# Cached keys and values in another tile shape: 32 blocks by four tokens in place of 96 blocks by one, in a two-layer decoder step

## The chip, the cores and the metric

One Trainium2 chip, one core. The metric is the device time of one launch in microseconds (us), median over runs. A core has five engines with instruction queues of their own: TensorE (PE; PEld are its weight loads), VectorE (DVE), ScalarE (ACT), GpSimd (POOL) and SyncE (SP), which issues nearly all DMAs of this kernel.

## What is computed

One step of a two-layer decoder trunk for a prompt (256 tokens) and for samples (8 batches of 4 tokens), width 1024, all float32. The first layer mixes tokens with gated linear attention, the second with dilated attention: 16 heads of 64, three groups that look 128 steps back at dilations 1, 4 and 16, joined by their softmax denominators. The sample tokens attend to a cache of 2048 earlier keys and values per batch (8 MB of each per batch) and to their own four.

```python
DIL_WINDOWS, DIL_DILATIONS = (128, 512, 2048), (1, 4, 16)

def dilated_group_sample(q, k_ctx, v_ctx, dil, steps, wb):
    T = q.shape[1]
    idx = wb + np.arange(T)[:, None] - dil * np.arange(steps + 1)[None, :]
    kg = k_ctx[:, idx]
    vg = v_ctx[:, idx]
    s = jnp.einsum('bthe,btjhe->bhtj', q, kg) * DIL_SCALE
    p, lse = masked_softmax(s, jnp.asarray(idx >= 0)[None, None])
    return jnp.einsum('bhtj,btjhe->bthe', p, vg), lse.transpose(0, 2, 1)
```

With dilation 16, token t of the four needs the cache rows 16 j + t for the blocks j = 0 to 127. So of each block of 16 rows four are read, and each of the four matters to one token only. The last 32 blocks lie in the last 512 rows, which dilation 4 reads in full.

## The kernel before

The program is one long sequence of stages: adaLN products, feed-forward, linear attention, feed-forward, the shared keys and values, feed-forward, queries, dilated attention, output product, feed-forward. Each weight product is three TensorE products of high and low halves (L554 to L556); the halves come from ScalarE (L183) and VectorE (L187).

Weights and caches come through one `Stream`. `job_list` writes down every load of the program in order. A job is cut into pieces of at most 128 x 1024 floats, and `pump` issues a DMA from SyncE for the next piece as long as fewer than RAW_BUFS = 11 pieces are loaded or in flight past the last one released. A consumer calls `take`, reads, and `free` releases the slots, in order; that lets `pump` issue more. A slot is reused, so an issue waits for those that read its last contents.

The change is in `dilated`, in the part for the sample tokens, about 1123 to 1321 us of the profiled execution. It runs over 16 steps x (and five more for what lags): four passes of two batches each (`it`, called `pr` in the helpers; `bp` is the batch of the two), and in each pass four steps (g, tp). g = 1 is the last 512 rows of the cache as 128 blocks of four rows, g = 2 the first 1536 rows as 96 blocks of 16 (J2 = 96); tp is 0 or 1. Group 0's keys lie within those of g = 1. In every step, per batch:

- `cache_job` (L329 on) made the load: two tokens u (2 tp and 2 tp + 1) of every block, each a piece of its own with a block per partition. That is 128 partitions (512 KB) for g = 1 and 96 (384 KB) for g = 2, and rows of 4 KB in both.
- `keys` turned the raw tiles with TensorE transposes (L1393), 8 chunks of 128 columns for each token, four transposes into one PSUM bank, and evacuated each bank into `kt`, by turns on ScalarE (L1513) and VectorE (L1511). GpSimd appended the sample's own key as a last column (L1517).
- `key_scores` multiplied the queries (`qz`, four row groups of 32: head half by batch) with `kt` (matmuls of L1390 into bank `pb`); VectorE then added them up in `Sc` through `tmask`, which keeps for each query row its own token (L1550, L1552).
- After the four steps of a pass, `softmax` normalized `Sc` and spread group 1's weights by token into the tile `W` (tag W1, one buffer). `weights` turned `W` (four transposes), `Pn` (the sample's own) and the 96 columns of `Sc` for g = 2, and VectorE spread the latter by token with the constant `ptmask` (L1589), in a `scratch` tile (named xh or xl).
- `outputs`, five steps later than the keys, multiplied these weights with the value tiles (L1390, out pa, 512 columns, two instructions each), four row groups for each token; `om` and `selz` collect the result in `pd`.

Between the parts of a step, `pieces` puts in small parts of the prompt's attention (tiles `pe`, `pT`). All transposes and matmuls in here are pinned to the order in which they are written, so PE runs in program order. The loads of a step x are the keys of step x and the values of step x - 5.

Of the kernel before, what the change touches and what calls it, by code (L numbers as in the profile page):

```python
# [18 lines left out]
P = 128  # L19
# [33 lines left out]
def host_constants():  # L53
    c = {}
    c["ident"] = np.eye(P, dtype=np.float32)
    half = 32
    inv = (10000.0 ** (-np.arange(half) / half)).astype(np.float32)
    pos = np.concatenate([np.arange(NP), np.tile(PAST + np.arange(TS), NB)]).astype(np.float32)
    ang = (inv[:, None].astype(np.float32) * pos[None, :]).astype(np.float32)
    cos, sin = np.cos(ang).astype(np.float32), np.sin(ang).astype(np.float32)  # L60
    t = np.stack([np.concatenate([cos, cos]), np.concatenate([-sin, sin])])
    c["rope"] = np.ascontiguousarray(np.tile(t, (1, 2, 1)).transpose(1, 0, 2))
    c["ropeq"] = c["rope"] * np.float32(0.125)
    i = np.arange(P)
# [35 lines left out]
    c["ptmask"] = np.broadcast_to((np.arange(32)[None, :] % TS == np.arange(TS)[:, None]), (P, TS, 32)).astype(np.float32).copy()  # L100
# [14 lines left out]
class Stream:  # L115
# [22 lines left out]
    def load(self, v, j, k0, nk):  # L138
        if j["kind"] == "first":
            for m in range(2):  # L140
                self.nc.sync.dma_start(v[:, :, 256 * m:256 * m + 256], j["src"][:, k0:k0 + nk, m])
        else:
            self.nc.sync.dma_start(v, j["src"][:, k0:k0 + nk, :])

# [186 lines left out]
def cache_job(I, name, g, b, tp, key):  # L331
    c = I[name][b].rearrange("s h e -> s (h e)")
    if g == 1:
        v = c[1536:2048, :].rearrange("(j t) f -> j t f", t=4)
    else:

        v = c.rearrange("(j t) f -> j t f", t=16)[0:J2]
    return dict(kind="r", key=key, src=v[:, 2 * tp:2 * tp + 2, :], nk=2, nc=D, rows=v.shape[0])


def body(tc, I, O, C, dbg=None):
# [1020 lines left out]
    def dilated(KT, Vt, Vs, xh, xl):  # L1362
# [134 lines left out]

        def keys(pr, g, tp, bp):

            n = P if g == 1 else J2  # L1500
            ji, _, raw = S.take(("K", g, pr, tp, bp))
            kt = [sp.tile([P, 4, 2, n + 1], F32, name=nm("kt"), tag=q, bufs=SPLIT_BUFS) for q in ("hi", "lo")]
            for c2 in range(4):
                pt = bankA().rearrange("p (f u j) -> p f u j", f=2, u=2)[:, :, :, 0:n]
                for f in range(2):
                    c = 2 * c2 + f
                    for u in range(2):
                        transpose(pt[:, f, u, :], raw[u][:, P * c:P * c + P], ident[0:n, 0:n])
                dst = kt[c2 // 2][:, 2 * (c2 % 2):2 * (c2 % 2) + 2, :, 0:n]
                if c2 % 2:  # L1510
                    V.tensor_copy(dst, pt)  # L1511
                else:
                    A.activation(dst, pt, AF.Copy)  # L1513
            S.free(ji)
            n0 = NP + TS * (2 * pr + bp) + 2 * tp
            for q in range(2):
                G.tensor_copy(kt[q][:, :, :, n], KT[:, 4 * q:4 * q + 4, n0:n0 + 2])  # L1517
            return kt

        def key_scores(g, tp, kc, qz, Sc):  # L1520
            n = P + 1 if g == 1 else N2
            ps = bankB()
            quarters = [(hp, bp) for hp in range(2) for bp in range(2)]

            for c4 in range(4):
                for kind in range(3 if g == 1 else 1):
                    for hp, bp in quarters:
                        c, q = 4 * hp + c4, 32 * (2 * bp + hp)
                        k_ = kc[bp][hp][:, c4]
# [9 lines left out]
            if g == 1:  # L1539
# [5 lines left out]
            for u in range(2):  # L1545
                t = 2 * tp + u
                for o_, m, s_ in [(132, 129, 129 * u), (261 + N2, 32, 324 + 32 * u)] if g == 1 else [(261, N2, N2 * u)]:
                    src, dst = ps[:, s_:s_ + m], Sc[:, o_:o_ + m]
                    if t == 0:
                        V.tensor_scalar(out=dst, in0=src, scalar1=ld["tmask"][:, 0:1], scalar2=None, op0=ALU.mult)  # L1550
                    else:
                        V.scalar_tensor_tensor(out=dst, in0=src, scalar=ld["tmask"][:, t:t + 1], in1=dst, op0=ALU.mult,  # L1552
                                               op1=ALU.add)
# [23 lines left out]
        def weights(Sc, W):  # L1577
            p1 = bankA()
            for t in range(TS):
# [2 lines left out]
            A.activation(W1, p1.rearrange("p (t x) -> p t x", t=TS), AF.Copy)  # L1582
# [163 lines left out]
```

## Time and profile before

| | |
|---|---|
| median of 3 runs | 1606.9 us (1605.67 to 1610.69) |
| the profiled execution | 1601.49 us |
| its span, mean granted TensorE clock | 1599.7 us, 0.979 |
| instructions | 31842 |
| DMA over the whole span | 342.75 MB, mean 214 GB/s |
| cache loads | 64 of 512 KB and 64 of 384 KB |

The profile is of one execution. "Busy" is the time in which an engine had an instruction running; the chain of work that ended last is followed back from the last instruction, step by step, to what released each. An idle time belongs to the instruction that came after it, and names what ended it. In a row such as "L1393 PE MATMUL pa<-ident,raw 96*128 96x96 f32 x256" stand the line, engine, operation, output and inputs, partitions by columns of the weights, the shape of the moving tile, and the count; busy us and mean ns of one follow.

### The profile page before, as it was taken

How to read it: one execution, taken by the hardware profiler on the slowest of the kernel's cores; microseconds unless marked ns; L12 is line 12 of the kernel's file. 1: busy time of each engine (PE TensorE's matmuls, PEld its weight loads, DVE VectorE, ACT ScalarE, POOL GpSimd, SP SyncE). 2: the span in 40 equal slices, each digit the busy share in tenths (PEclk: the TensorE clock that was granted, in tenths of full speed). 3: DMA queues.
4: the chain of work that ended last, by engine and by line, in shares of the span. 5: the costliest groups of instructions: out<-in, count | busy, mean ns of one | idle time of the engine just before them, and what ended most of it. 6: DMA issues, size and time to landing. Idle time of an engine off the chain costs nothing.

```text
span 1599.7 us, 31842 instructions
## 1 busy us (share of the span) xinstructions
PE 1506.4 (94%) x12794; PEld 1343.4 (84%) x12794; DVE 914.4 (57%) x1902; ACT 723.6 (45%) x1173; POOL 217.0 (14%) x367
## 2 busy tenths in 40 slices
PE   6999999999889999998999999898998988999996
PEld 4999998798868999987999999797755637899995
DVE  3644446596785444467544454666665667745556
ACT  2444334745644443346444433477443344544432
POOL 0000030102321000303000004032521112200001
PEclk8999999999999999999999999998999999999998
DMA  9966775644856678755676676643799998555430
GB/s 303 323 222 227 246 249 159 225 154 154 297 168 227 221 226 282 245 177 185 230 250 211 211 261 203 191 130 111 230 288 304 297 292 284 169 173 162 153 98 30
DMA packets 238822, 342.75 MB, mean 214 GB/s; under 512 B 12744, under 2 KB 202386, under 8 KB 238675
## 3 DMA queue, kind: packets, MB, share of 16 engines
q1 hardware_dynamic: 236210, 333.41, 65.6%
q0 software_dynamic: 2048, 7.14, 1.2%
q8 instruction: 100, 1.64, 0.4%
q14 instruction: 48, 0.39, 0.1%
q10 hardware_dynamic: 416, 0.17, 0.0%
HBM read 332.42 MB, written 8.26 MB: 213 GB/s over the span
## 4 chain that ended last, share of the span: by engine, by line
PE 73%; DMA 10%; DVE 8%; ACT 5%; issue 2%; POOL 1%; SPq 0%; DVEq 0%; ACTq 0%; POOLq 0%
PE pa L554 20%; PE pa L555 20%; PE pa L556 20%; DMA raw<-in_cache_k_dram 6%; PE pd L471 4%; DMA raw<-in_cache_v_dram 2%; DVE lo L187 2%; PE pa L1393 2%; PE pb L1390 1%; ACT xm L792 1%; ACT xm L1303 1%; PE pa L1051 1%; DVE z L694 1%; ACT hi L183 1%; ACT xh L800 1%
## 5 line engine op out<-in xcount | busy, mean ns | idle before, releaser
L554 PE MATMUL pa<-xh,hi 128*128 128x288 f32 x1868 | 548.3, 301 | 17.2 <-ACT xh L800 9.9
L556 PE MATMUL pa<-xh,lo 128*128 128x288 f32 x1868 | 554.2, 298 | 4.6 <-DVE lo L187 4.5
L555 PE MATMUL pa<-xl,hi 128*128 128x288 f32 x1868 | 555.2, 298 | 0.6 <-DVE xl L1663 0.4
L187 DVE TENSOR_TENSOR lo<-raw,hi 128x1024 fp32r<-128x1024 f32 (+2 forms) x365 | 424.1, 1170 | 227.6 <-ACT hi L183 225.2
L183 ACT ACTIVATE hi<-raw 128x1024 fp32r<-128x1024 f32 x350 | 358.7, 1035 | 254.9 <-PE pa L555 237.1
L554 PEld LDWEIGHTS pa<-xh,hi 128*128 128x128 f32 x1868 | 349.5, 190 | 38.1 <-ACT xh L800 18.3
L556 PEld LDWEIGHTS pa<-xh,lo 128*128 128x128 f32 x1868 | 356.0, 191 | 7.6 <-DVE lo L187 6.2
L555 PEld LDWEIGHTS pa<-xl,hi 128*128 128x128 f32 x1868 | 356.2, 191 | 1.1 <-DVE xl L1663 0.7
L554 PE MATMUL pa<-hh,hi 128*128 128x288 f32 x704 | 209.8, 298 | 0.0
L556 PE MATMUL pa<-hh,lo 128*128 128x288 f32 x704 | 208.9, 297 | 0.0
L555 PE MATMUL pa<-hl,hi 128*128 128x288 f32 x704 | 208.3, 296 | 0.0
L888 DVE TENSOR_TENSOR sa<-pa,sa 128x288 f32<-128x288 f32 x88 | 39.6, 454 | 181.8 <-PE pa L556 177.3
L554 PEld LDWEIGHTS pa<-hh,hi 128*128 128x128 f32 x704 | 132.8, 189 | 4.7 <-issue 2.9
L556 PEld LDWEIGHTS pa<-hh,lo 128*128 128x128 f32 x704 | 132.6, 188 | 0.2
L555 PEld LDWEIGHTS pa<-hl,hi 128*128 128x128 f32 x704 | 132.6, 188 | 0.1
L889 ACT ACTIVATE hh<-sa 128x288 fp32r<-128x288 f32 x88 | 38.7, 445 | 136.6 <-DVE sa L888 133.7
L887 ACT ACTIVATE sa<-pa 128x288 f32<-128x288 f32 x88 | 34.9, 401 | 97.6 <-PE pa L556 97.6
L1393 PEld LDWEIGHTS pa<-ident,raw 128*128 128x128 f32 (+1 forms) x512 | 53.3, 146 | 26.3 <-issue 8.1
L471 PE MATMUL pd<-raw,cT 128*32 128x256 f32 x1008 | 73.9, 385 | 1.3 <-ACT adas L479 1.3
L1393 PE MATMUL pa<-ident,raw 128*128 128x128 f32 (+1 forms) x512 | 63.7, 274 | 9.4 <-DMA raw<-in_cache_k_dram 4.6
L616 POOL TENSOR_TENSOR z<-z,lnpiv 128x288 f32<-128x288 f32 x6 | 4.7, 806 | 484.4 <-ACT lnpiv L611 484.4
L1513 ACT ACTIVATE kt<-pa 128x512 f32<-128x512 f32 (+1 forms) x64 | 34.0, 541 | 69.1 <-PE pa L1393 61.5
(381 smaller groups left out, 1756.1 us busy)
## 6 DMA issues: line engine op xcount, KB each, us to landing
raw<-in_w_ffn_up_dram SPq DMA_DIRECT2D x172, 512.0 KB, 6.1
raw<-in_w_ada_dram SPq DMA_DIRECT2D x110, 512.0 KB, 5.7
raw<-in_w_ffn_down_dram SPq DMA_DIRECT2D x80, 512.0 KB, 4.9
raw<-in_cache_k_dram SPq DMA_DIRECT2D x32, 512.0 KB, 7.3
raw<-in_cache_v_dram SPq DMA_DIRECT2D x32, 512.0 KB, 10.6
raw<-in_w_in_a_dram SPq DMA_DIRECT2D x24, 512.0 KB, 4.8
raw<-in_w_q_b_dram SPq DMA_DIRECT2D x24, 512.0 KB, 3.7
raw<-in_cache_k_dram SPq DMA_DIRECT2D x32, 384.0 KB, 10.6
```

The costliest lines, as they stand in the source:

```text
L183: self.pin("act", self.nc.scalar.activation(hv, src, AF.Copy))
L187: self.pin("dve", self.nc.vector.tensor_tensor(out=lo[:, k, :], in0=src[:, k, :], in1=hv[:, k, :].bitcast(F32), op=ALU.subtract))
L471: x = T.matmul(ps[32 * q:32 * q + 32, :], lhsT=cT[:, k, :], rhs=raw[kk][:, 256 * q:256 * q + 256], start=(k == 0), stop=(k == DC - 1), til ...
L554: ins = [T.matmul(ps, lhsT=whi, rhs=xhi, start=first, stop=False), T.matmul(ps, lhsT=whi, rhs=xlo, start=False, stop=False), T.matmul(ps, ...
L555: T.matmul(ps, lhsT=whi, rhs=xlo, start=False, stop=False),
L556: T.matmul(ps, lhsT=wlo, rhs=xhi, start=False, stop=last)]
L694: pin("dve", V.tensor_tensor(out=z[:, c, :], in0=z[:, c, :], in1=self.rstd, op=ALU.mult))
L887: A.activation(sa, pa[:, 0:NT], AF.Silu)
L888: V.tensor_tensor(out=sa, in0=pu[:, 0:NT], in1=sa, op=ALU.mult)
L889: A.activation(hh[:, m, :], sa, AF.Copy)
L1393: pin("pe", T.transpose(*a))
L1513: A.activation(dst, pt, AF.Copy)
```

## The change

Group 2's loads take another shape. A tile now holds 32 blocks by their first four rows, so its 128 partitions are (block, token) pairs, 512 KB in runs of 16 KB. The 96 blocks of a batch make three tiles: step tp = 0 takes the first two, step tp = 1 the third. The bytes are the same; four pieces of 96 partitions become three of 128, for keys and for values, and 128 cache loads become 112.

In `keys` a bank then holds two chunks of two tiles (tp = 0) or four chunks of one (tp = 1), and the batch's own four keys are appended once, at tp = 1. In `key_scores` the columns of a step are 256 and 132 in place of 194 and 194; a column's token is its index modulo 4, so VectorE adds four strided parts of 64 or 33 columns per step, in place of two of 97. In `weights` VectorE first spreads the 96 columns of `Sc` by token with `tmask` into a new tile `w2` with tag W1, PE turns its three parts, and VectorE copies them to the `scratch` tile. `outputs` runs over three value tiles where it ran over four tokens. The constant `ptmask` and its load are gone. Group 1 is as before.

```diff
+        elif "tiles" in j:
+            self.nc.sync.dma_start(v[:, 0, :], j["tiles"][k0])
...
-        v = c.rearrange("(j t) f -> j t f", t=16)[0:J2]
-    return dict(kind="r", key=key, src=v[:, 2 * tp:2 * tp + 2, :], nk=2, nc=D, rows=v.shape[0])
+        return dict(kind="r", key=key, src=v[:, 2 * tp:2 * tp + 2, :], nk=2, nc=D)
+    v = c.rearrange("(j t) f -> j t f", t=16)
+    tiles = [v[32 * i:32 * i + 32, 0:TS, :] for i in ((0, 1) if tp == 0 else (2,))]
+    return dict(kind="r", key=key, tiles=tiles, nk=len(tiles), nc=D)
...
-            n = P if g == 1 else J2
-            kt = [sp.tile([P, 4, 2, n + 1], F32, name=nm("kt"), tag=q, bufs=SPLIT_BUFS) for q in ("hi", "lo")]
-            for c2 in range(4):
-                pt = bankA().rearrange("p (f u j) -> p f u j", f=2, u=2)[:, :, :, 0:n]
...
+            nu, n = len(raw), P + (0 if (g, tp) == (2, 0) else TS if g == 2 else 1)
+            kt = [sp.tile([P, 4, nu, n], F32, name=nm("kt"), tag=q, bufs=SPLIT_BUFS) for q in ("hi", "lo")]
+            nf = 4 // nu
+            for c2 in range(DC // nf):
+                pt = bankA().rearrange("p (f u j) -> p f u j", f=nf, u=nu)
...
+                parts = [(t, 261 + 64 * tp, ps[:, t:nc_:TS]) for t in range(TS)]
+            for t, o_, src in parts:
+                dst = Sc[:, o_:o_ + src.shape[1]]
...
-            transpose(pt[0:J2, P:2 * P], Sc[:, 261:261 + J2], ident)
-            W2 = scratch[1][0:J2, 1536:2048].rearrange("p (q t x) -> p q t x", q=4, t=TS)
-            V.tensor_tensor(out=W2, in0=bc(pt[0:J2, P:2 * P].rearrange("p (q x) -> p q x", q=4), 2, TS),
-                            in1=bc(ld["ptmask"][0:J2], 1, 4), op=ALU.mult)
+            w2 = tile("W1", [P, TS, P])[:, 0:3, :]
+            V.tensor_tensor(out=w2.rearrange("p i (j t) -> p (i j) t", t=TS), in0=bc(Sc[:, 261:261 + J2], 2, TS),
+                            in1=bc(ld["tmask"], 1, J2), op=ALU.mult)
+            for i in range(3):
+                transpose(pt[:, P * i + P:P * i + 2 * P], w2[:, i, :], ident)
+            W2 = scratch[1][:, 1536:1536 + 3 * P].rearrange("p (i x) -> p i x", i=3)
+            V.tensor_copy(W2, pt[:, P:4 * P].rearrange("p (i x) -> p i x", i=3))
...
-                    for u in range(2):
+                    for u in range(len(rr[0][2])):
...
-                            mm(po[32 * gr:32 * gr + 32, :], lhsT=W1[:, t, 32 * gr:32 * gr + 32] if g == 1 else W2[:, gr, t, :],
+                            mm(po[32 * gr:32 * gr + 32, :], lhsT=(W1 if g == 1 else W2)[:, t, 32 * gr:32 * gr + 32],
```

SyncE's queue in the second pass, where the keys of step (2, 1) and the values of step (2, 0) of the pass before are issued. The number in a name only tells the tiles apart. Before:

```order
L143 DMA raw_12963<-in_cache_v_dram 128x1024
L143 DMA raw_12965<-in_cache_k_dram 96x1024
L143 DMA raw_12967<-in_cache_k_dram 96x1024
L143 DMA raw_12969<-in_cache_k_dram 96x1024
L143 DMA raw_12997<-in_cache_k_dram 96x1024
L143 DMA raw_12999<-in_cache_v_dram 96x1024
L143 DMA raw_13114<-in_cache_v_dram 96x1024
L143 DMA raw_13116<-in_cache_v_dram 96x1024
L143 DMA raw_13128<-in_cache_v_dram 96x1024
L143 DMA raw_13130<-in_cache_k_dram 128x1024
```

The same place now:

```order
L144 DMA raw_12937<-in_cache_v_dram 128x1024
L142 DMA raw_12939<-in_cache_k_dram 128x1x1024
L142 DMA raw_12941<-in_cache_k_dram 128x1x1024
L142 DMA raw_12943<-in_cache_v_dram 128x1x1024
L142 DMA raw_12971<-in_cache_v_dram 128x1x1024
L142 DMA raw_12973<-in_cache_v_dram 128x1x1024
L142 DMA raw_13086<-in_cache_v_dram 128x1x1024
L144 DMA raw_13088<-in_cache_k_dram 128x1024
```

Four key tiles of 96 partitions became two of 128; of the values this step still takes four, and the step after takes two.

PE's queue at `weights`, with the semaphores that an instruction waits for. Before:

```order
L1393 MATMUL pa_13571<-ident,pe_13234 128x128 x2
L1393 MATMUL pa_13577<-ident,W_916_13337 128x128 [waits DVE_49]
L1393 MATMUL pa_13577<-ident,W_916_13337 128x128 x3
L1393 MATMUL pa_13583<-ident,Pn_12243 128x128 [waits Activation_49]
L1393 MATMUL pa_13583<-ident,Sc_12664 96x128
L1390 MATMUL pd_12242<-om_13427,c_selz_11195 32x256 x4
L1390 MATMUL pa_13593<-raw_13298,xh_12235 32x512 [waits DMAHW0_49,DVE_49,Activation_49]
```

Now, where `W_939` is the tile w2:

```order
L1396 MATMUL pa_13509<-ident,pe_13178 128x128 x2
L1396 MATMUL pa_13515<-ident,W_908_13283 128x128 [waits DVE_49]
L1396 MATMUL pa_13515<-ident,W_908_13283 128x128 x3
L1396 MATMUL pa_13521<-ident,Pn_12241 128x128 [waits Activation_49]
L1396 MATMUL pa_13521<-ident,W_939_13525 128x128 [waits DVE_49,Activation_49]
L1396 MATMUL pa_13521<-ident,W_939_13525 128x128 x2
L1393 MATMUL pd_12240<-om_13365,c_selz_11193 32x256 x4
L1393 MATMUL pa_13535<-raw_13211,xh_12233 32x512 [waits DMAHW1_49]
```

The one transpose of `Sc`, without a wait, became three of w2, and the first of them waits for VectorE.

VectorE's queue at the same place. Before:

```order
L1511 COPY kt_13533<-pa_13541 128x4x128 [waits PE_49]
L1511 COPY kt_13534<-pa_13553 128x4x128 [waits PE_49]
L1589 TENSOR_TENSOR xl_12236<-pa_13583,c_ptmask_11191 96x512 [waits Activation_49]
L1511 COPY kt_13610<-pa_13618 128x4x96 [waits PE_49]
L1511 COPY kt_13611<-pa_13630 128x4x96 [waits PE_49]
```

Now:

```order
L1516 COPY kt_13471<-pa_13479 128x4x128 [waits PE_49]
L1516 COPY kt_13472<-pa_13491 128x4x128 [waits PE_49]
L1604 TENSOR_TENSOR W_939_13525<-Sc_12632,c_tmask_11187 128x384 [waits PE_49]
L1609 COPY xl_12234<-pa_13521 128x384 [waits PE_49,Activation_49]
L1516 COPY kt_13552<-pa_13560 128x512 [waits PE_49]
L1516 COPY kt_13553<-pa_13572 128x512 [waits PE_49]
```

One masked product of the turned weights became a product ahead of PE's transposes, which waits for PE, and a copy behind them; two kt copies stand ahead of it.

More of the change, by code (lines that the diff above doesn't have):

```diff
@@ L99, in host_constants @@
     c["rmask"] = np.repeat((i[:, None] // 64 == np.arange(2)[None, :]).astype(np.float32)[:, :, None], TS, axis=2)
-    c["ptmask"] = np.broadcast_to((np.arange(32)[None, :] % TS == np.arange(TS)[:, None]), (P, TS, 32)).astype(np.float32).copy()
     c["blkmask"] = ((i[:, None] % 32) // TS == np.arange(512)[None, :] // 64).astype(np.float32)
@@ L334, in cache_job @@
         v = c[1536:2048, :].rearrange("(j t) f -> j t f", t=4)
-    else:
-        v = c.rearrange("(j t) f -> j t f", t=16)[0:J2]
-    return dict(kind="r", key=key, src=v[:, 2 * tp:2 * tp + 2, :], nk=2, nc=D, rows=v.shape[0])
+        return dict(kind="r", key=key, src=v[:, 2 * tp:2 * tp + 2, :], nk=2, nc=D)
+    v = c.rearrange("(j t) f -> j t f", t=16)
+    tiles = [v[32 * i:32 * i + 32, 0:TS, :] for i in ((0, 1) if tp == 0 else (2,))]
+    return dict(kind="r", key=key, tiles=tiles, nk=len(tiles), nc=D)
 def body(tc, I, O, C, dbg=None):
@@ L1379, in dilated @@
         ld = {}
-        for n, sh in (("g0mask", [P, TS, 33]), ("tmask", [P, TS]), ("rmask", [P, 2, TS]), ("ptmask", [P, TS, 32]),
+        for n, sh in (("g0mask", [P, TS, 33]), ("tmask", [P, TS]), ("rmask", [P, 2, TS]),
                       ("blkmask", [P, 512]), ("selz", [P, 4, 2, NS])):
@@ L1498, in keys @@
         def keys(pr, g, tp, bp):
-            n = P if g == 1 else J2
             ji, _, raw = S.take(("K", g, pr, tp, bp))
-            kt = [sp.tile([P, 4, 2, n + 1], F32, name=nm("kt"), tag=q, bufs=SPLIT_BUFS) for q in ("hi", "lo")]
-            for c2 in range(4):
-                pt = bankA().rearrange("p (f u j) -> p f u j", f=2, u=2)[:, :, :, 0:n]
-                for f in range(2):
-                    c = 2 * c2 + f
-                    for u in range(2):
-                        transpose(pt[:, f, u, :], raw[u][:, P * c:P * c + P], ident[0:n, 0:n])
-                dst = kt[c2 // 2][:, 2 * (c2 % 2):2 * (c2 % 2) + 2, :, 0:n]
+            nu, n = len(raw), P + (0 if (g, tp) == (2, 0) else TS if g == 2 else 1)
[3 more added lines that the diff above has]
+                pt = bankA().rearrange("p (f u j) -> p f u j", f=nf, u=nu)
+                for f in range(nf):
+                    c = nf * c2 + f
+                    for u in range(nu):
+                        transpose(pt[:, f, u, :], raw[u][:, P * c:P * c + P], ident)
+                c0 = nf * c2
+                dst = kt[c0 // 4][:, c0 % 4:c0 % 4 + nf, :, 0:P]
                 if c2 % 2:
@@ L1514, in keys @@
             S.free(ji)
-            n0 = NP + TS * (2 * pr + bp) + 2 * tp
-            for q in range(2):
-                G.tensor_copy(kt[q][:, :, :, n], KT[:, 4 * q:4 * q + 4, n0:n0 + 2])
+            n0 = NP + TS * (2 * pr + bp)
+            if n > P:
+                for q in range(2):
+                    if g == 1:
+                        G.tensor_copy(kt[q][:, :, :, P], KT[:, 4 * q:4 * q + 4, n0 + 2 * tp:n0 + 2 * tp + 2])
+                    else:
+                        G.tensor_copy(kt[q][:, :, 0, P:n], KT[:, 4 * q:4 * q + 4, n0:n0 + TS])
             return kt
         def key_scores(g, tp, kc, qz, Sc):
-            n = P + 1 if g == 1 else N2
+            nc_ = kc[0][0].shape[2] * kc[0][0].shape[3]
             ps = bankB()
@@ L1530, in key_scores @@
                         if kind == 0:
-                            mm(ps[q:q + 32, 0:2 * n], lhsT=qz[:, g, c, bp, :], rhs=k_.rearrange("p u j -> p (u j)"),
+                            mm(ps[q:q + 32, 0:nc_], lhsT=qz[:, g, c, bp, :], rhs=k_.rearrange("p u j -> p (u j)"),
                                start=(c4 == 0), stop=(c4 == 3 and g == 2), tile_position=(0, q))
@@ L1544, in key_scores @@
                 V.tensor_tensor(out=Sc[:, P + 2 * tp:P + 2 * tp + 2], in0=s0[:, :, 32], in1=m0[:, :, 32], op=ALU.add)
[L1545 to L1553, printed above, removed]
+            parts = []
+            if g == 1:
+                for u in range(2):
+                    t = 2 * tp + u
+                    parts += [(t, 132, ps[:, 129 * u:129 * u + 129]), (t, 261 + N2, ps[:, 324 + 32 * u:356 + 32 * u])]
+            else:
+                parts = [(t, 261 + 64 * tp, ps[:, t:nc_:TS]) for t in range(TS)]
+            for t, o_, src in parts:
+                dst = Sc[:, o_:o_ + src.shape[1]]
+                if t == 0:
+                    V.tensor_scalar(out=dst, in0=src, scalar1=ld["tmask"][:, 0:1], scalar2=None, op0=ALU.mult)
+                else:
+                    V.scalar_tensor_tensor(out=dst, in0=src, scalar=ld["tmask"][:, t:t + 1], in1=dst, op0=ALU.mult,
+                                           op1=ALU.add)
         def softmax(pr, Sc):
@@ L1598, in outputs @@
                     rr = [S.take(("V", g, pr, tp, bp)) for bp in range(2)]
-                    for u in range(2):
+                    for u in range(len(rr[0][2])):
                         t = 2 * tp + u
```

## The prediction

> **What bounds the kernel now.** I read the page first: what is busy, and the chain of work that ended last.
>
> ```profile
> PE 1506.4 (94%) x12794; PEld 1343.4 (84%) x12794; DVE 914.4 (57%) x1902; ACT 723.6 (45%) x1173; POOL 217.0 (14%) x367
> PE 73%; DMA 10%; DVE 8%; ACT 5%; issue 2%; POOL 1%; SPq 0%; DVEq 0%; ACTq 0%; POOLq 0%
> PE pa L554 20%; PE pa L555 20%; PE pa L556 20%; DMA raw<-in_cache_k_dram 6%; PE pd L471 4%; DMA raw<-in_cache_v_dram 2%; DVE lo L187 2%; PE pa L1393 2%; PE pb L1390 1%; ACT xm L792 1%; ACT xm L1303 1%; PE pa L1051 1%; DVE z L694 1%; ACT hi L183 1%; ACT xh L800 1%
> ```
>
> On average TensorE bounds, but 8 of the 10% that the chain gives to DMA are cache loads, and only one stage has those, 1123 to 1321 us. So its own chain comes next (start, length, what), then SyncE's timeline.
>
> ```profile
> 1187.66 11.70 DMA raw<-in_cache_k_dram
> ...
> 1223.94 11.29 DMA raw<-in_cache_k_dram
> ...
> 1235.27 3.91 PE pa L1393 x19
> 1239.18 11.32 DMA raw<-in_cache_k_dram
> ...
> 1302.38 12.03 DMA raw<-in_cache_v_dram
> ...
> 1314.45 1.91 PE pa L1390 x12
> 1264.43 38.26 SPq L143 DMA_DIRECT2D raw<-in_cache_v_dram  x24
> ```
>
> Ten DMA links fill 1187.66 to 1314.41 but for 3.9 us. The last row has 24 issues in 38.26 us, 1.59 each, so a link of about 12.4 us is eight transfers deep: an issue waits until the transfer eight before it has landed. Ten links are 80 transfers in 126.8 us. Here the end is set by **how fast cache tiles land**. The windows view says how far behind PE is: the four rounds of four steps, then narrow windows in which only 512 KB tiles were in flight (three), only 96-row tiles (fourth), and a change from the one to the other (fifth). The columns I use are length, PE busy, DVE busy (third) and, last, GB/s.
>
> ```profile
> 1139.20:1187.30 48.10, 46.89 (x688) 33.98 (x686) 31.17 (x103) 19.23 (x42) 12.12 (x46) 1.00 0.96 301
> 1187.30:1235.20 47.90, 43.09 (x529) 26.07 (x525) 28.30 (x107) 17.32 (x39) 13.34 (x42) 1.00 1.03 305
> 1235.20:1276.40 41.20, 38.79 (x489) 26.43 (x493) 23.95 (x86) 14.36 (x32) 4.85 (x17) 0.96 1.03 299
> 1276.40:1320.80 44.40, 37.23 (x304) 15.65 (x296) 29.60 (x119) 18.03 (x42) 7.45 (x12) 0.96 1.05 290
> sum 181.60, PE 166.00 PEld 102.14 DVE 113.02 ACT 68.95 POOL 37.77; mean PE 41.50 PEld 25.53 DVE 28.26 ACT 17.24 POOL 9.44
> 1197.00:1205.00 8.00, 7.62 (x129) 4.70 (x124) 5.45 (x15) 2.39 (x6) 4.17 (x15) 1.00 1.03 408
> 1245.00:1252.00 7.00, 7.00 (x84) 3.86 (x86) 5.72 (x23) 1.20 (x2) 0.00 (x0) 1.00 1.03 406
> 1288.00:1295.00 7.00, 6.22 (x50) 3.44 (x50) 4.99 (x28) 0.42 (x2) 0.00 (x0) 1.00 1.03 408
> 1279.00:1286.00 7.00, 6.52 (x67) 2.95 (x65) 6.37 (x21) 4.53 (x12) 2.49 (x4) 1.00 1.02 262
> 1297.00:1301.00 4.00, 2.45 (x20) 0.32 (x12) 3.75 (x10) 1.75 (x6) 2.02 (x3) 1.00 1.07 202
> ```
>
> A 512 KB tile (0.524 MB) lands every 0.524/408 = **1.29 us**; a 384 KB tile (0.393 MB) takes 0.393/262 = **1.50 us**, more for three quarters of the bytes. But PE is busy 166.0 of 181.6 us: it is right behind.
>
> **The change part by part.**
>
> *Loads.* In a full round 32 DMAs become 28, all of 128 partitions, over the same bytes. If the new tiles land like group 1's, a round needs 28 x 1.29 = 36.1 us, and the 80 transfers above, half of them of 96 rows, become 70, 90 us for 126.8. PE needs 41.5 us a round on average, so the bound passes to PE, and the gain is not 36 us but what PE loses to cache DMAs today. The waits view over the stage gives it (total, times, longest); weight loads run beside matmuls.
>
> ```profile
> PEld pa L1390 <- DMA raw<-in_cache_v_dram: 17.1, 13, 2.8
> PE pa L1390 <- DMA raw<-in_cache_v_dram: 6.9, 9, 1.9
> PEld pa L1393 <- DMA raw<-in_cache_k_dram: 5.1, 6, 1.4
> PE pa L1393 <- DMA raw<-in_cache_k_dram: 4.6, 6, 1.2
> ```
>
> Matmul idle is 6.9 + 4.6 = 11.5, weight-load idle 17.1 + 5.1 = 22.2; part of the second lies under matmuls still running. Taking 0.3 us of cover for each of the 19 waits, half of a 0.6 us matmul, gives 16.5, between the two. Some first waits remain: I leave 2. **-14.5 us** (-9.5 to -22.2).
>
> One rule speaks against this saving. The Trainium skill, "SBUF — State Buffer", section "Summary: rules for kernel authors", says to estimate transfers from HBM at about 358 GB/s. By that figure a tile would take an estimated 1.46 us and a round 41.0, as long as PE; half the waits staying, the change would be worth about -7. The trace disagrees: 406 to 408 in three windows.
>
> *TensorE work.* Rows by form, columns count | busy, mean ns.
>
> ```profile
> L1393 PE MATMUL pa<-ident,raw 128*128 128x128 f32 x256 | 35.7, 295 | 4.5 <-DVE lnsq L1304 2.4 <-DMA raw<-in_cache_k_dram 1.2 <-ACT kt L1513 0.8
> L1393 PE MATMUL pa<-ident,raw 96*128 96x96 f32 x256 | 28.3, 254 | 4.8 <-DMA raw<-in_cache_k_dram 3.3 <-DVE kt L1511 0.9 <-ACT kt L1513 0.5
> L1390 PE MATMUL pa<-raw,xh 128*32 128x512 f32 x128 | 16.8, 599 | 3.4 <-DMA raw<-in_cache_v_dram 2.9 <-ACT xh L1582 0.5
> L1390 PE MATMUL pb<-kt,xl 128*32 128x194 f32 x128 | 6.6, 330 | 0.0
> L1390 PE MATMUL pb<-kt,xh 128*32 128x258 f32 x128 | 10.4, 391 | 0.0
> L1390 PE MATMUL pb<-kt,xh 128*32 128x66 f32 x128 | 4.9, 220 | 0.0
> L1393 PE MATMUL pa<-ident,W 128*128 128x128 f32 x16 | 2.6, 283 | 0.0
> ```
>
> Transposes: 256 of 96 columns, 28.3, become 192 of 128 at 35.7/256 = 0.139, 26.8: -1.5. V products: 128 become 96, at 16.8/128 = 0.131: -4.2. Scores: as many instructions, 2 x 194 columns becoming 256 + 132. By columns that costs nothing. By the nearest rows, 256 costs 10.4/128 = 0.081, and 132, halfway between 66 (0.038) and 194 (0.052), 0.045; 128 x (0.081 + 0.045 - 2 x 0.052) = +2.8. I take +1, nearer to equal columns. Weights: two transposes more per pass, eight in all, +1.1. Together **-3.6 us** (-4.6 to -1.8).
>
> *The new wait.* Before, group 2's weights went through one transpose of Sc, whose operand was long ready. Now VectorE writes w2 over W, which it may do only when PE's four transposes of W have ended (283 ns each, in flight), and PE then waits for w2. The rows here are VectorE's.
>
> ```profile
> L1566 DVE TENSOR_TENSOR W<-Sc,c_tmask 128x512 f32<-128x512 f32 x4 | 2.7, 685 | 0.0
> L1511 DVE COPY kt<-pa 128x512 f32<-128x512 f32 x32 | 21.7, 686 | 14.0 <-PE pa L1393 13.7
> L1511 DVE COPY kt<-pa 128x384 f32<-128x384 f32 x32 | 17.4, 554 | 15.0 <-PE pa L1393 14.1 <-ACT kt L1513 0.6 <-POOL kt L1517 0.2
> L1552 DVE SCALAR_TENSOR_TENSOR Sc<-pb,c_tmask,Sc 128x97 f32<-128x97 f32 x12 | 3.8, 319 | 2.9 <-PE pb L1390 2.7
> L1552 DVE SCALAR_TENSOR_TENSOR Sc<-pb,c_tmask,Sc 128x32 f32<-128x32 f32 x12 | 2.9, 241 | 0.0
> ```
>
> The 384-wide product is 685 x 384/512 = 0.51 us; with the 0.28 ahead of it 0.8, or 1.5 if a kt copy (0.69) stands ahead in VectorE's queue. Four passes: +3.2 to +6; I take **+4 us**, since the copy ahead was released by earlier transposes and should mostly be done. PE's queue is in order: the selz products, the next V products and transposes stand behind, and for those ScalarE's and VectorE's evacuations wait.
>
> *VectorE, ScalarE, GpSimd.* Score evacuation: 16 operations of 97 columns, 5.1 us, become 16 of 64 and 16 of 33 in chains of four, near the 241 ns row, some 0.26 each: 8.3, +3.2. kt copies: 24 x 0.686 = 16.5 for 17.4. w2 and its copy: 4 x (0.51 + 0.55) = 4.2 for four masked products of 0.68, +1.5. Net +3.8 on 113.0 of 181.6 us. VectorE idles 38% of the stage, so I cost it **0**, or +3.8 if the cover is gone: the chain of four ends a step, and softmax waits for it once a pass. ScalarE has eight fewer evacuations, GpSimd fewer key columns to append; both idle more than VectorE: 0. The mask's DMA (64 KB) and SyncE's 16 fewer issues lie ahead of or beside this work: 0.
>
> Sum: -14.5 - 3.6 + 4 = **-14 us**, own time 1601.5 to 1587.5; the span is 1599.7, and 1.8 lie around it. The median of the runs, 1606.9, is 5.4 above the profiled execution; less the same 14, it becomes **1593**. All favourable ends: -22.2 - 4.6 + 3.2 = -23.6, 1583. All unfavourable: -9.5 - 1.8 + 6 + 3.8 = -1.5, 1605.
>
> **The rivals.**
>
> *Slower: the tiles land badly.* The new source is 32 blocks of four rows, a form that the trace lacks. If its 512 KB land at the 202 GB/s of the changing window, one takes 2.6 us: 48 x 2.6 = 124.8 for 64 x 1.50 = 96, +29, **1636**. It decides above 96/48 = 2.0 us a tile (262 GB/s), then DMA stays the bound and grows. For it: 96-row tiles already land slower than size explains. Against: destination and row length are group 1's. By the Trainium skill, "DMA: Bandwidth & Descriptors", section "Why a DMA increments its semaphore by 16 and not by 1", a DMA uses the largest number of engines up to 16 that divides both sides' slowest dimension: here 32 and 128, so all 16. No run shows it yet. 0.07.
>
> *Same.* The new tile lands at 262 GB/s per byte, so group 2's loads take 96 us as now, or PE's waits for cache only turn into waits for evacuations and w2: about **1606**. For it: in the busiest round PE idles 1.2 us in 48.1. Against: the later rounds idle 2.4 to 7.2 us, mostly on cache. 0.11.
>
> *More.* DMA is the only bound, and PE's busy time is stretched by its waiting: -36.8, **1570**. Against: 166.0 of 181.6. 0.08.
>
> **How the numbers follow.** The forecast has 0.74, its own range 1583 to 1605. 1578 to 1606 leaves out the slower rival, most of the larger gain and part of "same", under 0.2. A measurement here can tell 0.3%, 4.8 us. Faster: 0.71 of the forecast and 0.08 = 0.79; same: 0.03 of it and 0.10 = 0.13; slower 0.07 + 0.01 = 0.08.
>
> **What would show it.** Right: GB/s windows near 400 throughout, no DMA links left in this stage's chain, the four DMA waits at some 2 us, a wait of PE for W of about 1 us four times, PE's busy time in the rounds at 160 to 166 with the stage about 14 us shorter. Wrong: DMA links between 1187 and 1300 as before (tile cost), or PE waiting for kt evacuations as long as it did for cache.

## The result, and the profile after

| | before | after |
|---|---|---|
| median | 1607.57 us (1605.67 to 1610.69, 4 runs) | 1593.87 us (1590.77 to 1595.59, 4 runs) |
| ratio, 95% interval | | 0.9911, 0.9886 to 0.9935 |
| the profiled execution, its span | 1601.49, 1599.7 us | 1592.31, 1589.8 us |

The change makes the kernel 0.9% faster, 13.7 us by the medians. The two profiled executions differ by less, 9.9 us in their spans, and where the time went can be read only from these. The page of the profile after, its first part and the chain that ended last:

```profile
span 1589.8 us, 31589 instructions
PE 1493.8 (94%) x12706; PEld 1335.9 (84%) x12706; DVE 915.4 (58%) x1914; ACT 722.8 (45%) x1165; POOL 215.0 (14%) x351
PE 76%; DVE 9%; ACT 5%; issue 4%; DMA 3%; POOL 2%; SPq 0%; DVEq 0%; POOLq 0%; ACTq 0%
PE pa L557 20%; PE pa L558 19%; PE pa L559 19%; PE pd L474 3%; PE pa L1396 3%; PE pb L1393 3%; DVE lo L188 2%; PE pa L1393 2%; ACT xm L1306 1%; PE pa L1054 1%; POOL xm L1308 1%; ACT xm L795 1%; POOL ax L708 1%; DVE z L697 1%; DMA raw<-in_w_q_b_dram 1%
```

The 8% of cache loads have left the chain; transposes (L1396) and products (L1393) of the same stage stand in their place. What TensorE waits for in the stage now, in the waits view (us in total, times, longest):

```profile
PEld pa L1393 <- DMA raw<-in_cache_v_dram: 1.4, 5, 0.3
PE pa L1396 <- DVE W L1604: 4.7, 2, 3.5
PE pa L1396 <- DVE sm L1417: 1.0, 1, 1.0
PE pa L1396 <- ACT PT L1601: 0.7, 1, 0.7
PE pa L1396 <- DVE pe L1425: 10.1, 5, 7.6
```

Of the waits for cache DMAs, 11.5 us at matmuls and 22.2 at weight loads before, 1.4 us at weight loads are left. But new ones have come: 6.4 us at w2 (the three rows after the first), and 10.1 for the prompt's softmax, 7.6 of it in one piece behind the last value product. PE's timeline shows that piece, before (first four rows) and after (the others):

```profile
1314.92 1.45 PE L1390 MATMUL pa<-Vs,PT 128*32 128x512 f32 x6
1316.30 0.55 PE L1393 MATMUL pa<-ident,pe 128*128 128x128 f32 x3
1319.78 0.64 PE L1390 MATMUL pd<-om,c_selz 128*32 128x256 f32 x8
1322.77 0.40 PE L554 MATMUL pa<-xh,hi 128*128 128x288 f32 x1
...
1299.42 1.04 PE L1393 MATMUL pa<-Vs,PT 128*32 128x512 f32 x8
1308.09 1.98 PE L1396 MATMUL pa<-ident,pe 128*128 128x128 f32 x6 [7.63 <-DVE pe L1425]
1310.01 2.25 PE L1393 MATMUL pa<-pT,Vt 128*64 128x256 f32 x8
1312.19 1.08 PE L1393 MATMUL pd<-om,c_selz 128*32 128x256 f32 x8
1315.01 0.40 PE L557 MATMUL pa<-xh,hi 128*128 128x288 f32 x1
```

Before, the last prompt softmax was done by the time the values had landed: its transposes follow the last value product at once. Now the values are done 16 us earlier in the span and TensorE waits for that softmax. In four stretches (to the first key transposes; from there to the last value product; from there to the output product; the rest) the spans are:

| us | before | after | before, tiles padded (see below) |
|---|---|---|---|
| to the first key transposes | 1123.1 | 1120.7 | 1121.4 |
| keys and values | 193.3 | 179.7 | 176.5 |
| to the output product | 6.4 | 14.6 | 10.2 |
| the rest | 276.9 | 274.8 | 277.1 |

The code ahead of the stage is the same in all of them, but for the mask's load, so I put 2.4 of the 9.9 us down to scatter. Keys and values gained 13.6 us, the end of the stage gave 8.2 back, and the rest won 2.1: before, the output product ran at half clock from 1324.2 to 1327.6 us, and now the spell of half clock is over by 1313.6 us, ahead of it. So 8.2 and 2.1 belong together.

### The profile page after: what moved, and what is told of

It is laid out like the page before. It is cut to its first block, busy times and chain, and to the rows that moved or that the text cites. A ratio compares the mean times of both kernels' runs of the same rounds, so it can differ in the third digit from the quotient of the medians.

```text
span 1589.8 us, 31589 instructions
## 1 busy us (share of the span) xinstructions
PE 1493.8 (94%) x12706; PEld 1335.9 (84%) x12706; DVE 915.4 (58%) x1914; ACT 722.8 (45%) x1165; POOL 215.0 (14%) x351
## 4 chain that ended last, share of the span: by engine, by line
PE 76%; DVE 9%; ACT 5%; issue 4%; DMA 3%; POOL 2%; SPq 0%; DVEq 0%; POOLq 0%; ACTq 0%
PE pa L557 20%; PE pa L558 19%; PE pa L559 19%; PE pd L474 3%; PE pa L1396 3%; PE pb L1393 3%; DVE lo L188 2%; PE pa L1393 2%; ACT xm L1306 1%; PE pa L1054 1%; POOL xm L1308 1%; ACT xm L795 1%; POOL ax L708 1%; DVE z L697 1%; DMA raw<-in_w_q_b_dram 1%
## 5 line engine op out<-in xcount | busy, mean ns | idle before, releaser
L557 PEld LDWEIGHTS pa<-xh,hi 128*128 128x128 f32 x1868 | 347.8, 189 | 39.4 <-ACT xh L803 18.5
L1396 PEld LDWEIGHTS pa<-ident,raw 128*128 128x128 f32 x448 | 49.8, 144 | 19.8 <-issue 7.7
L1518 ACT ACTIVATE kt<-pa 128x512 f32<-128x512 f32 x56 | 32.8, 595 | 67.6 <-PE pa L1396 55.6
L1396 PE MATMUL pa<-ident,raw 128*128 128x128 f32 x448 | 59.3, 283 | 4.4 <-DVE lnsq L1307 2.4
```

The lines of the kernel that those rows point to most:

```text
L557: ins = [T.matmul(ps, lhsT=whi, rhs=xhi, start=first, stop=False), T.matmul(ps, lhsT=whi, rhs=xlo, start=False, stop=False), T.matmul(ps, ...
L1396: pin("pe", T.transpose(*a))
```

## The experiments

Ratios are to the kernel before, which was run again beside each group of runs; medians in us.

| run | median | ratio, 95% interval |
|---|---|---|
| the changed kernel again | 1593.47 | 0.9915, 0.9896 to 0.9934 |
| group 2's tiles loaded as 96 + 32 partitions | 1622.31 | 1.0103, 1.0066 to 1.0139 |
| before, tiles padded to 128 partitions | 1587.29 | 0.9885, 0.9857 to 0.9913 |
| before, tiles padded to 112 partitions | 1622.47 | 1.0079, 1.0045 to 1.0114 |
| keys new, values old and padded | 1587.56 | 0.9878, 0.9857 to 0.9898 |
| values new, keys old and padded | 1595.84 | 0.9931, 0.9911 to 0.9951 |
| after, w2 early | 1590.22 | 0.9903, 0.9875 to 0.9931 |
| the same, w2's transposes in their own bank | 1586.88 | 0.9873, 0.9840 to 0.9906 |
| the same, prompt one step earlier | 1583.15 | 0.9850, 0.9816 to 0.9883 |
| after, prompt one step earlier | 1595.20 | 0.9921, 0.9893 to 0.9948 |
| keys new, prompt one step earlier | 1588.75 | 0.9886, 0.9852 to 0.9919 |
| after, splits late | 1592.84 | 0.9913, 0.9892 to 0.9934 |

**Is it the landing of the tiles?** My theory was that the gain comes from how fast a tile lands; the rival was that TensorE and the evacuations have less to do. One run takes the landing away and keeps the work, the other the reverse.

```diff
-            self.nc.sync.dma_start(v[:, 0, :], j["tiles"][k0])
+            x = j["tiles"][k0]
+            self.nc.sync.dma_start(v[0:96, 0, :], x[0:24])
+            self.nc.sync.dma_start(v[96:128, 0, :], x[24:32])
```

> The changed kernel, only that each of group 2's tiles is loaded by two DMAs, one of 96 partitions (24 blocks) and one of 32 (8 blocks). Bytes, tiles and all work of the engines are those of the changed kernel. Theory L (what counts is how fast a tile lands): if a 96-partition DMA keeps its 1.50 us and the 32-partition one takes at least 0.131 MB / 262 GB/s = 0.5 us, a tile takes 2.0 us, a round 16 x 1.29 + 12 x 2.0 = 44.6 us, over the 39 us in which PE is busy; DMA links come back into the stage's chain and most of the gain goes: 1603 to 1615 us. Rival W (the gain comes from the smaller work of TensorE and of the evacuations): 1590 to 1598, as the changed kernel.

```diff
-        v = c.rearrange("(j t) f -> j t f", t=16)[0:J2]
+        v = c.rearrange("(j t) f -> j t f", t=16)
...
-                        transpose(pt[:, f, u, :], raw[u][:, P * c:P * c + P], ident[0:n, 0:n])
+                        transpose(pt[:, f, u, :], raw[u][0:n, P * c:P * c + P], ident[0:n, 0:n])
...
-                               rhs=rr[bp][2][u][:, 512 * hp:512 * hp + 512], start=(g == 1 and t == 0), stop=False,
+                               rhs=rr[bp][2][u][0:P if g == 1 else J2, 512 * hp:512 * hp + 512], start=(g == 1 and t == 0), stop=False,
```

> The kernel before, only that group 2's loads take all 128 blocks of a token in place of 96, so 512 KB by 128 partitions; the last 32 partitions are not read by anything. Work of the engines is that of before, and 8 MB more are moved. Theory L: a tile lands in 1.29 us in place of 1.50, a round needs 32 x 1.29 = 41.3 us for 47.9, about what PE is busy (41.5 on average); the kernel gets faster by 8 to 14 us: 1594 to 1600. Rival W (work of the engines): 1604 to 1611, no change. Rival B (bytes at the 300 GB/s of the rounds): 8.4 MB / 300 = 28 us more, 1636.

Split in two, the same tiles and the same work gave 1622.3, slower than before and past what I expected; in this run's trace cache DMAs are back in the chain and TensorE's matmuls wait 14.6 us for them. This run also has 48 loads more than the changed kernel, so by itself it doesn't tell partitions from the number of loads; the padded run does. Padded, with all work as before and 8 MB more to move, the kernel reached 1587.3: better than I expected, and 6.6 us better than the change (1585.94 to 1588.42 beside 1590.77 to 1595.59, the single runs). So the landing is the whole gain, and the rest of the change costs. The windows view of the padded run, in three stretches (GB/s last):

```profile
1196.00:1204.00 8.00, 6.54 (x128) 4.30 (x120) 5.82 (x17) 2.86 (x8) 4.44 (x14) 1.00 1.03 409
1236.00:1244.00 8.00, 8.00 (x74) 4.82 (x76) 6.70 (x26) 2.73 (x7) 0.00 (x0) 1.00 1.02 407
1260.00:1268.00 8.00, 8.00 (x96) 4.69 (x96) 4.49 (x21) 1.55 (x4) 0.00 (x0) 1.00 1.03 410
```

and of the changed kernel:

```profile
1198.00:1205.00 7.00, 6.16 (x99) 4.35 (x87) 6.85 (x24) 2.48 (x5) 0.32 (x2) 1.00 1.02 400
1228.00:1234.00 6.00, 5.67 (x73) 4.27 (x73) 4.42 (x18) 3.32 (x8) 0.58 (x4) 1.00 1.03 414
```

Rows of 4 KB from 128 blocks (padded) and runs of 16 KB from 32 blocks (changed) land alike, at 400 to 414 GB/s. The changed kernel's stretches hold tiles of group 1 too; the landing times in its trace have four new key tiles behind each other at 1202.59, 1203.87, 1205.14 and 1206.40 us, 1.27 us apart. It is the 128 partitions that matter, not the longer runs.

**Is it 96, or anything under 128?**

```diff
-        v = c.rearrange("(j t) f -> j t f", t=16)
+        v = c.rearrange("(j t) f -> j t f", t=16)[0:112]
```

> The kernel before, only that group 2's loads take 112 blocks of a token in place of 96 (448 KB by 112 partitions, 0.459 MB); the last 16 partitions are not read by anything. What is open is whether a tile lands slowly because it is 96 partitions, or because it is fewer than 128. If a tile of fewer than 128 partitions costs as much per row as the 96-row one (1.50 us / 96 = 15.6 ns), it takes 1.75 us, a round 16 x 1.29 + 16 x 1.75 = 48.6 us for 47.9: 1605 to 1612. By the Trainium skill, SBUF - State Buffer, section Door 1 (the DMA port swizzle), the ports that partitions 0 to 63 reach carry eight rows each with 96, 112 and 128 partitions alike, so a tile of 112 would take what one of 128 does, 1.29 us: then TensorE bounds, as in the run with 128 blocks, 1585 to 1591.

The run was slower than the kernel before, 14 us by the medians, more than I had put. In a stretch in which tiles of 112 were landing, its windows view has

```profile
1282.00:1294.00 12.00, 9.01 (x96) 5.19 (x90) 6.04 (x27) 3.64 (x10) 0.92 (x2) 1.00 1.03 266
```

266 GB/s, so 0.459/266 = 1.72 us a tile, near the 1.75 of the price per row; 96 partitions had 262. 64 tiles at 1.72 - 1.50 = 0.22 us more are 14 us, so the estimate by tiles meets the loss. My 48.6 us for a round were held against the wrong number: the same sum gives 44.6 for a round before, which took 47.9. Of the sizes tried, only 128 has the full rate. The rule by ports, in which 112 costs what 128 does, does not hold here.

**Which half costs?** Each half of the new shape by itself, with padded tiles for the other.

```diff
+    if name == "cache_v":
+        return dict(kind="r", key=key, src=v[:, 2 * tp:2 * tp + 2, :], nk=2, nc=D)
     tiles = [v[32 * i:32 * i + 32, 0:TS, :] for i in ((0, 1) if tp == 0 else (2,))]
```

(keys new; `weights` and `outputs` are those of before)

> Keys and scores as in the changed kernel; values and weights as in the kernel before, with value tiles padded to 128 blocks as in the padded run. So the loads all have 128 partitions, and only the keys' part of the new shape is there. The padded run (both parts old) had 1587.3, the changed kernel (both new) 1593.9, 6.6 more; 3.7 of these went when w2 was made early. Theory K (the other 3 are the four dependent score additions of VectorE per step and the wider score columns): 1589 to 1592. Rival V (all of the loss is in the values' part): 1584 to 1588, the fewer transposes and evacuations being worth 0 to 3 us.

```diff
+    if name == "cache_k":
+        return dict(kind="r", key=key, src=v[:, 2 * tp:2 * tp + 2, :], nk=2, nc=D)
     tiles = [v[32 * i:32 * i + 32, 0:TS, :] for i in ((0, 1) if tp == 0 else (2,))]
```

(values new; `keys` and `key_scores` are those of before)

> Values and weights as in the changed kernel (w2 over W, three tiles); keys and scores as in the kernel before, with key tiles padded to 128 blocks. Theory K: the w2 wait alone shows, and 1.0 to 4 us of saved value products stand against it: 1586 to 1591. Rival V: 1591 to 1595, as the changed kernel.

The rival was right: keys new costs nothing (1584.58 to 1588.26, where the changed kernel, run beside it, had 1590.52 to 1594.45), values new has all of the loss. The second run is even slower than the changed kernel, and its trace has a longer stretch at half clock behind w2 (third from last in the windows view), 6 us where the changed kernel, below, has 3:

```profile
1257.00:1263.00 6.00, 5.84 (x31) 2.11 (x32) 0.57 (x2) 0.00 (x0) 0.00 (x0) 0.50 0.32 93
```

**What w2 costs.** In the third pass, TensorE (first and last row) and VectorE of the changed kernel, by the timeline:

```profile
1249.31 0.88 PE L1396 MATMUL pa<-ident,W 128*128 128x128 f32 x3 [3.51 <-DVE W L1604]
...
1247.43 1.27 DVE L1516 COPY kt<-pa 128x512 f32<-128x512 f32 x2
1248.63 0.54 DVE L1604 TENSOR_TENSOR W<-Sc,c_tmask 128x384 f32<-128x384 f32 x1
...
1250.12 1.08 PE L1393 MATMUL pd<-om,c_selz 128*32 128x256 f32 x8
```

VectorE had run through the prompt's softmax, which waited for ScalarE and GpSimd on its way, and two kt copies before it came to w2. TensorE stood for 3.51 us. Then it worked slowly: its selz products took 1.08 us, 0.64 elsewhere. The windows view has the granted clock (third from last):

```profile
1247.00:1249.00 2.00, 0.00 (x0) 0.00 (x0) 2.00 (x6) 0.00 (x0) 0.00 (x0) 0.94 0.89 348
1249.00:1250.00 1.00, 0.69 (x3) 0.50 (x3) 0.17 (x1) 0.00 (x0) 0.00 (x0) 0.50 0.67 274
1250.00:1251.00 1.00, 1.00 (x13) 0.42 (x16) 0.56 (x1) 0.00 (x0) 0.00 (x0) 0.50 0.09 37
1251.00:1252.00 1.00, 1.00 (x12) 0.34 (x8) 0.00 (x0) 0.00 (x0) 0.00 (x0) 0.50 0.06 16
1252.00:1253.00 1.00, 1.00 (x16) 0.14 (x8) 0.00 (x0) 0.00 (x0) 0.00 (x0) 0.91 0.00 0
```

From 1249 to 1252 TensorE ran at half clock: some 3 us, half of them lost, so 1.5 us on top of the wait. The first run forms w2 at the end of `softmax`, in a place of its own:

```diff
-            w2 = tile("W1", [P, TS, P])[:, 0:3, :]
+            w2 = scratch[1][:, 1536 + 3 * P:1536 + 6 * P].rearrange("p (i x) -> p i x", i=3)
```

(and its product with `tmask` stands in `softmax`, after the one of `W`)

> The changed kernel, only that w2 has a place of its own (in the free end of a scratch tile), and that VectorE forms it at the end of softmax, four PE steps ahead of the transposes that read it. The theory that the new wait costs what PE's waits at w2 say (4.7 us for w2 in two passes, 1.0 behind a reduction in another): these go and the time falls by 3 to 6 us to 1588 to 1591. Rival: PE's order then waits for the kt copies that stand in the same queue of VectorE, and nothing is won: 1592 to 1596.

The waits for w2 went, and the half clock in that pass with them; the median is 3.3 us below that of the changed kernel run again, though the two intervals overlap. The gain stands where the waits were: keys and values took 174.9 us, 179.7 in the changed kernel. One wait was left, 0.7 us in each pass:

```profile
PE pa L1396 <- ACT PT L1604: 2.9, 4, 0.7
```

w2's transposes go into the bank that ScalarE reads PT from. So the second run gives them their own:

```diff
+            p2 = bankA()
             for i in range(3):
-                transpose(pt[:, P * i + P:P * i + 2 * P], w2[:, i, :], ident)
+                transpose(p2[:, P * i:P * i + P], w2[:, i, :], ident)
...
-            V.tensor_copy(W2, pt[:, P:4 * P].rearrange("p (i x) -> p i x", i=3))
+            V.tensor_copy(W2, p2[:, 0:3 * P].rearrange("p (i x) -> p i x", i=3))
```

> The changed kernel with w2 early in a place of its own, as in the run before, and its three transposes in a PSUM bank of their own, so that they do not wait for ScalarE to read the bank that they shared with the transposed Pn (0.7 us in each of four passes, ACT PT in the waits of that run). Theory (the values' part costs only what PE waits at w2, and the half clock after a wait of over 3 us): no wait at w2 is left, none of the half-clock spell behind it, and the time falls from 1590.2 by some 2 to 3 us to 1587 to 1588.5, level with the run that keeps the old values' part. Rival (the rest of the values' part costs too: a loss of its own of some 3 us): 1589.5 to 1591.

The median, 1586.88, lies just below the theory's range (runs 1583.83 to 1588.95), level with the padded kernel and below every run of the changed one, though the intervals of the ratios overlap a little (0.9840 to 0.9906 and 0.9896 to 0.9934). No wait for w2 or PT is left in the trace. But keys and values took 175.3 us, no less than in the run before; in the two traces the stage is shorter at its end, 11.3 for 14.3 us. So what this second wait cost by itself is not shown, only what the two repairs are worth together.

**The end of the stage.** Two causes were possible for the 7.6 us: the latency of the last prompt softmax, or the splits of the output weights, which stand ahead of it on ScalarE and VectorE and wait there for their DMA:

```profile
1299.34 1.06 ACT L184 ACTIVATE hi<-raw 128x1024 fp32r<-128x1024 f32 x1 [3.86 <-DMA raw<-in_w_out_b_dram]
```

```diff
-START = 5
+START = 4
```

> The changed kernel, only that the pieces of the prompt's attention begin one step earlier (START 4 for 5), so three pieces fewer are left for the end. Theory: PE's idle time of 7.6 us ahead of the last prompt transposes is the latency of the last prompt softmax, which the waits for value tiles covered before; with the pieces earlier it lies beside value products again, and the time falls by 4 to 8 us to 1586 to 1590. Rival: the idle time comes from the splits of the output weights, which stand ahead of that softmax in the queues of ScalarE and VectorE and wait for their DMAs; then it stays, or moves, and the time is 1592 to 1597.

For the second, the last prompt exponential and the last scaling are put ahead of the splits in the fixed order of their engines:

```diff
-        self.prep(i + (self.jobs[i]["kind"] != "first"))
+        self.prep(i + (self.jobs[i]["kind"] != "first" and key[0] != "V"))
...
+                    if (c, t) == (DC - 1, 1) and e is hs[1][0]:
+                        pin("act", z_)
...
+                    if (c, t) == (DC - 1, 1) and e is hs[1][0]:
+                        pin("dve", z_)
```

> The changed kernel, only that the splits of the output weights on ScalarE and VectorE are ordered behind the last prompt softmax. Theory S (of the 14 us between the last value product and the output product, 4 come from splits that wait for their DMA at the head of these queues): the last prompt transposes come 3 to 4 us earlier, the output product starts that much earlier and then runs slower for some 2 us; the time falls by 1 to 3 us to 1590 to 1593. Rival (the latency of that softmax itself, about 5 us from its scores to its transposes, and the splits have to be done anyway): within 1 us of the changed kernel.

Neither won anything clear of the noise by itself. With the splits late, TensorE's wait for the softmax fell from 10.1 to 4.9 us, and the output product began 3.1 us earlier (1313.56, 1316.66 in the changed kernel run again), but it then ran at half clock until 1318.8 us. So some 4 to 5 us of that wait are the splits, and the rest is the softmax. With the prompt earlier, the end fell from 14.6 to 3.2 us, as the theory had it, but keys and values took 193.4 us for 179.7: the waits moved into them, 3.3 us for w2 and 4.0 for PT among them, and 27 us at half clock in place of 14. That is the rival's case. Then the earlier prompt on the kernel with w2 repaired, and on the one with the old values' part:

> The same, and the prompt's pieces one step earlier (START 4). With the waits at w2 gone, value products follow the last prompt softmax, and the idle time and the half clock between the last value product and the output product (13 to 14 us in the changed kernel) shrink: 1583 to 1586. Rival, as in the changed kernel with START 4: the pieces only move the waits to other places, 1587 to 1590.

> The run with the keys' part new and the old values' part on padded tiles (1587.6), and the prompt's pieces one step earlier (START 4). If the end of the stage is what is left to win, 1583 to 1586; if the pieces only move the waits, 1587 to 1590.

The first had the lowest median of all, 1583.15. From its last value product to the output product it takes 3.2 us, 14.6 in the changed kernel, and keys, values and this end together 185.4, 194.3 in the changed kernel. Against the run without the earlier prompt it is 3.7 us by the medians, and the two intervals overlap (0.9816 to 0.9883 and 0.9840 to 0.9906); in the traces its stage is 1.2 us shorter (186.6 there): 8.1 less at the end, 6.9 more in keys and values. The second won nothing: its end fell from 10.2 to 3.8 us, and keys and values rose from 175.5 to 184.7. So an earlier prompt mostly moves the waits; that it wins anything is not shown.

## Why the prediction was right, and where its terms were not

The direction, the mechanism (faster landing passes the bound from DMA to TensorE) and the size were right: 1593 forecast, 1593.87 measured. Its terms were less so.

*Loads: -14.5, measured -18.* The padded kernel has this term alone: 18.5 us by the medians, though 8 MB more are moved, and with the longer end of its stage (+3.8) inside. My step "the gain is what PE loses to cache DMAs" left out that TensorE also ran at half clock behind such waits. Before, the windows view has two stretches in sequence, and a third later on:

```profile
1228.00:1235.00 7.00, 4.61 (x29) 1.61 (x29) 2.46 (x9) 0.98 (x2) 0.59 (x3) 1.00 1.03 312
1235.00:1239.00 4.00, 3.73 (x19) 3.73 (x20) 1.02 (x2) 1.20 (x2) 0.00 (x0) 0.57 1.04 296
1303.00:1308.00 5.00, 5.00 (x32) 3.03 (x30) 1.20 (x8) 1.36 (x3) 0.00 (x0) 0.66 1.03 252
```

Busy 4.61 of 7 us, then four at 0.57 clock, 1.7 us lost; I had put such busy time down as work. This stretch is the link of 3.91 us of TensorE (x19) in the chain that the prediction shows. The third row loses another 1.7 us, but a DMA link of the chain runs beside it. The padded kernel has no half clock between 1133 and 1303 us. So 1.7 us of the 4 that I missed are shown; the others are not accounted for.

*TensorE work: -3.6, measured -4.9.* Rows by form after, to be held against those of the prediction:

```profile
L1396 PE MATMUL pa<-ident,raw 128*128 128x128 f32 x448 | 59.3, 283 | 4.4 <-DVE lnsq L1307 2.4 <-ACT kt L1518 1.7 <-DVE kt L1516 0.2
L1393 PE MATMUL pa<-raw,xh 128*32 128x512 f32 x128 | 15.7, 615 | 0.0
L1393 PE MATMUL pa<-raw,xl 128*32 128x512 f32 x96 | 12.8, 639 | 0.0
L1396 PE MATMUL pa<-ident,W 128*128 128x128 f32 x28 | 5.1, 302 | 6.7 <-DVE W L1604 4.7 <-DVE sm L1417 1.0 <-ACT PT L1601 0.7
```

Against the padded kernel, whose TensorE does the old work without cache waits, its rows for the transposes and the value products being

```profile
L1393 PE MATMUL pa<-ident,raw 128*128 128x128 f32 x256 | 35.2, 293 | 4.7 <-DVE lnsq L1304 2.4 <-DVE kt L1511 1.5 <-ACT kt L1513 0.8
L1393 PE MATMUL pa<-ident,raw 96*128 96x96 f32 x256 | 27.8, 253 | 1.6 <-DVE kt L1511 1.0 <-ACT kt L1513 0.4
L1390 PE MATMUL pa<-raw,xl 96*32 96x512 f32 x128 | 15.4, 598 | 0.0
L1390 PE MATMUL pa<-raw,xh 128*32 128x512 f32 x128 | 15.2, 598 | 0.5 <-ACT xh L1582 0.5
```

the groups compare as follows: transposes 59.3 for 63.0, -3.7 (forecast -1.5); value products 28.5 for 30.6, -2.1 (forecast -4.2; part of them ran at half clock, as the means of 615 and 639 ns show, 598 in the padded run); scores 12.2 for 12.7, -0.5 (forecast +1); transposes for weights 5.1 for 3.7, +1.4 (forecast +1.1). Together -4.9 beside -3.6.

*The new wait: +4, measured +6.4 of waits, and the half clock.* The forecast had about 1 us four times; it was 3.5 us once and less in the other passes. I had two kt copies ahead of w2 at the most, and took it that they "should mostly be done". What stood ahead was the prompt's softmax chain with its own waits, and the transposes' bank was a second wait that my reading of the order (its row names ScalarE too) passed over. Taking both away was worth 6.6 us by the medians (1593.47 to 1586.88), a part of it at the end of the stage.

*VectorE, ScalarE, GpSimd: 0.* That holds for the keys' part: with it alone the kernel has the padded one's time, 1587.56 and 1587.29. VectorE's score parts took 283 and 250 ns, and 0.26 us for each had been the estimate.

*Left out: the end of the stage.* For the waits that go, I asked what is late next only inside the rounds, not behind the last value product. When the waits for values went, the last prompt softmax lost its cover, +8.2 us in the changed kernel, 6.1 with the 2.1 that the output product then won. The gain of the loads, larger than forecast, and this loss nearly cancelled; that the sum came out within 1 us is partly luck.

The rivals: "slower" asked for tiles over 2.0 us, and the new tile has 1.27 to 1.31 (0.524 MB by 414 and 400 GB/s). "Same" came true in one piece, the waits at w2. "More" (1570) fell, since TensorE was busy through most of the stage; the best version found has 1583.

## What to carry to other kernels

Where loads of fewer than 128 partitions set the pace, try them with all 128, even if some of what they bring is not used: here the padded version moves 8 MB more and is faster than the reshaped one. When a wait goes, list what else was hidden under it, above all the last work of a second stream that was woven in. A small operand that TensorE will wait for is made where its inputs become ready, not where it is used, and not into a bank that another engine still reads.

## What was not expected of the hardware

- A tile of 96 or 112 partitions lands at 262 to 266 GB/s, one of 128 at 400 to 414, with rows of 4 KB or runs of 16 KB alike. From 112 to 96 the rate did not fall with the count. No other size was tried, and why 128 is faster stays open.
- TensorE's granted clock halves after a stretch with too little work, and the spells of half clock come in pieces of about 3.4 us: from 1100 to 1340 us all traces here have spells of 3.4, 6.8, 10.2 or 13.7 us and none in between. In the changed kernel the one at w2 lasts from 1248.8 to 1252.2 us, and the one behind the last value product from 1303.4 to 1313.6.
- No single long gap is needed. At w2 TensorE stood for 3.5 us, and the clock fell 3.0 us into that gap. Before the change it fell after 7 us in which TensorE was busy for 4.61 in pieces, with no gap over 1.2 us. In the padded kernel it fell with no gap over 1.4 us:

```profile
1298.00:1299.00 1.00, 0.00 (x0) 0.00 (x0) 0.88 (x3) 1.00 (x5) 0.70 (x2) 1.00 1.10 348
1299.00:1300.00 1.00, 0.30 (x1) 0.14 (x1) 0.96 (x3) 0.73 (x2) 0.63 (x3) 1.00 1.10 348
1300.00:1301.00 1.00, 0.41 (x2) 0.20 (x2) 0.96 (x4) 0.24 (x1) 0.69 (x1) 1.00 1.10 347
1301.00:1302.00 1.00, 0.30 (x1) 0.14 (x1) 0.96 (x4) 1.00 (x2) 0.00 (x0) 1.00 1.10 349
1302.00:1303.00 1.00, 0.90 (x4) 0.39 (x4) 1.00 (x2) 0.59 (x3) 0.00 (x0) 1.00 1.10 347
1303.00:1304.00 1.00, 0.94 (x5) 0.53 (x5) 0.69 (x1) 1.00 (x2) 0.00 (x0) 0.51 1.10 348
```

The Trainium skill, "TensorE: Matmul & The Clock Gate", section "What's actually happening", has the halving after an idle window of about 3.4 us. The case of w2 is near it; the other two show that TensorE need not be idle throughout. How little work is too little is not shown: before the change 2.06 us of busy time in the 3.41 us ahead of the fall were too little, and in the padded kernel 2.02 us in 3.41 (1296.19 to 1299.60) were enough.
